# One buffer for both tiles' candidates and the expert numbers, in a decoder layer on one Trainium2 core

## The chip, the core and the metric

The kernel runs on one core of a Trainium2 chip. Its engines each work through a queue of their own, in order: PE (TensorE, the matmuls; its weight loads are listed as PEld), DVE (VectorE), ACT (ScalarE), POOL (GpSimd, which here mostly issues indirect DMAs) and SP, which issues the large DMAs. The metric is the device time of one execution in microseconds (us); smaller is better.

## The reference

One decoder layer over 256 tokens of width 1024: a mixer (gated linear attention and block attention in parallel), and behind it a PEER channel mixer, which the change is in. PEER scores each token against 2 x 128 sub-keys in 8 heads, keeps the best 16 of each half, forms the sums of these pairs, keeps the best 16 of the sums, and with that has 128 experts for each token, of 16,384. The output adds, for each expert, gate times gelu(u_e . x) times v_e.

```python
sv, si = lax.top_k(s, PEER_TOPK)
cand = (sv[:, :, 0, :, None] + sv[:, :, 1, None, :]).reshape(T, PEER_HEADS, 256)
cand_id = (si[:, :, 0, :, None] * PEER_NKEYS + si[:, :, 1, None, :]).reshape(T, PEER_HEADS, 256)
top_s, pos = lax.top_k(cand, PEER_TOPK)
expert = jnp.take_along_axis(cand_id, pos, axis=-1)
gate = jax.nn.softmax(top_s, axis=-1)
# for each token t: sum over its 128 experts of gate * gelu(u_tab[e] . x_t) * v_tab[e]
```

## The kernel before

The tokens are treated in two ways. For tokens 96 to 255 ("many", ND = 160) the kernel multiplies with the whole tables: all 128 blocks of U and then all 128 blocks of V are streamed through TensorE, 512 KB a block (below: a piece), and the product with U is masked by the gates. For tokens 0 to 95 ("few", NS = 96) it gathers only the rows that are needed: 96 indirect DMAs of 512 KB for U and 96 for V, issued by POOL, and one DVE instruction on each.

**Retrieval.** The 256 tokens are two tiles of 128. For each tile `work[tt]` lists the steps on DVE: the best 16 of each half (16 calls of `top16`, each made of MAX, MAX_INDEX, MATCH_REPLACE, MAX, MAX_INDEX, L598 to L602), the pair sums into the tile `cand` (`pairs`, L610 and L613), the best 16 of the sums for each head (8 calls of `top16`, which read and rewrite `cand`), `gates` (a subtraction on DVE, L677, then an exponential on ACT, L678), `ranks` (L622 to L630), for each half `slots` to `slots3` (L637 to L655, ending in the index tile `ij`), and `gates2` (L683 to L685). After the first tile's slots `experts` makes the expert numbers `num` (L669, L670), which POOL writes to DRAM (L566) and reads back spread over the partitions (`ixs`, L573). Only then can POOL issue the gathers (L751), since they take their row numbers from `ixs`. Five buffers (`rowsof`) hold gathered rows. DVE frees one with L759 (U rows) or L769 (V rows). The second tile's retrieval feeds no gather; it is needed by the masks of the many tokens (L801 to L822), which begin at block pair J0 = 31 of U.

**U and V.** In pair `jp` of U TensorE fills one of two PSUM banks named `mm` (L120, two pieces), and ACT empties it with a gelu (L849). So pair jp + 2 cannot begin before ACT has emptied the bank of pair jp. ACT's exponential and its gelu need different function tables, so that a table load (ACT_TABLE_LOAD) stands ahead of each change. Index transposes (L660) and gate transposes (L692) stand between TensorE's matmuls. With V (L890) TensorE sums into three other banks, emptied once at the end (L912). SP fetches pieces in advance into a ring of 14 buffers.

**What sets the order.** The program is written in the order of `work` and of the pairs, and a scheduler then fixes each engine's own order, from the dependencies and from which buffers are free. Buffers come from pools: tiles with the same tag share the pool's slots, and a tile that takes a slot over must wait until every instruction on the tile before it is done, DMAs too. The pool `tk` has one slot for each tag. A tile without a tag goes by its name. So before the change the two `cand` tiles share one slot already, and `num` has a slot of its own.

Of the kernel before, what the change touches and what calls it, by code (L numbers as in the profile page):

```python
# [9 lines left out]
F32 = mybir.dt.float32  # L10
# [3 lines left out]
U32 = mybir.dt.uint32  # L14
# [6 lines left out]
NT = S // 128  # L21
# [8 lines left out]
SLOTS = 128  # L30
# [5 lines left out]
def layer(ctx: ExitStack, tc: tile.TileContext, a):  # L36
# [487 lines left out]
    tk = tk_ctx.enter_context(tc.tile_pool(name="tk", bufs=1))  # L524
# [38 lines left out]
    def to_parts(dst, name, src, cols):  # L563

        there = nc.dram_tensor(name, (NS, src.shape[1]), src.dtype, kind="Internal").ap()
        gp.dma_start(there, src)  # L566
        for l, (t0, n, m) in enumerate(FEW):
            rows = there[t0:t0 + n]
            if cols:
                rows = rows.rearrange("t (m w) -> m t w", m=m)  # L570
            else:
                rows = rows[None].to_broadcast([m, n, src.shape[1]])
            gp.dma_start(dst(l), rows)  # L573

    def by_part(dst):
        return lambda l: dst[:, FEW[l][0]:FEW[l][0] + FEW[l][1]]
# [13 lines left out]
    top = tk.tile([128, NT, 8, 16], F32, name="top")  # L590
    pos = tk.tile([128, NT, 8, 16], U32, name="pos")
    ij = tk.tile([128, 2, NT, 8, 16], F16, name="ij")
    cands = [tk.tile([128, 8, 112], F32, name="cand") for _ in range(NT)]
    later = []
    at = 0

# [7 lines left out]
    def pairs(tt):  # L604


        s0 = sv[:, tt, 0::2]
        s1 = sv[:, tt, 1::2]
        cd = cands[tt]
        ve.tensor_tensor(cd[:, :, 0:64].rearrange("p h (a b) -> p h a b", a=4),  # L610
                         s0[:, :, 0:4, None].to_broadcast([128, 8, 4, 16]),
                         s1[:, :, None, :].to_broadcast([128, 8, 4, 16]), op=OP.add)
        ve.tensor_tensor(cd[:, :, 64:112].rearrange("p h (a b) -> p h a b", a=12),  # L613
                         s0[:, :, 4:16, None].to_broadcast([128, 8, 12, 4]),
                         s1[:, :, None, 0:4].to_broadcast([128, 8, 12, 4]), op=OP.add)
# [47 lines left out]

    def experts():

        num = tk.tile([128, SLOTS], U32, name="num")
        r, c = (ij[:, w, 0].rearrange("p h k -> p (h k)") for w in range(2))
        numf = tk.tile([128, SLOTS], F32, name="numf")
        ve.scalar_tensor_tensor(numf, c, 128.0, r, op0=OP.mult, op1=OP.add)  # L669
        ve.tensor_copy(num, numf)  # L670
        to_parts(by_part(ixs), "experts", num[0:NS], True)
# [33 lines left out]
    for tt in range(NT):  # L705
        w_ = work[tt]
        w_.append((1.8, lambda tt=tt: pairs(tt)))
        w_ += [(1.6, lambda tt=tt, h=h: top16(top[:, tt, h], pos[:, tt, h], cands[tt][:, h])) for h in range(8)]
        st = {}
        w_.append((0.5, lambda tt=tt: gates(tt)))  # L710
        w_.append((3.0, lambda tt=tt, st=st: st.update(ab=ranks(tt))))
        for w in range(2):
            w_.append((1.8, lambda tt=tt, w=w, st=st: st.update(r=slots(tt, w, st["ab"]))))
            w_.append((2.4, lambda st=st: slots2(*st["r"])))
            w_.append((3.0, lambda tt=tt, w=w, st=st: slots3(tt, w, st["r"][0])))
        if tt == 0:
            w_.append((0.6, experts))
        w_.append((0.9, lambda tt=tt: gates2(tt)))
# [264 lines left out]
```

## Time and profile before

| what | us |
|---|---|
| median of 3 runs | 817.42 (817.12 to 818.36) |
| the profiled execution, its own time | 815.44 |
| span of the profiled execution | 813.7 |
| PE busy, share of the span | 98% |
| DVE busy | 61% |
| ACT, POOL busy | 30%, 28% |
| mean granted TensorE clock, as a share of 2.4 GHz | 0.988 |
| DMA over the span | 270 MB, 332 GB/s |

All positions below are us from the start of the span. The retrieval lies at about 160 to 270, the pairs of U at about 200 to 499, V from there to the end. A timeline row gives an instruction's start and length, how many equal ones are merged (x8), and in brackets how long its engine stood idle before it and what it then waited for. Instructions overlap a little, so the step from one start to the next is what one costs in a row. A busy PE is not a PE at its peak, since the ends of matmuls are modelled.

### The profile page before, as it was taken

To read this page: it belongs to the slowest core of one execution; us is meant where nothing else is said; L and a number is where in the kernel's file an instruction comes from. 1 tells how busy PE (TensorE), PEld (TensorE's weight loads), DVE (VectorE), ACT (ScalarE), POOL (GpSimd) and SP (SyncE) were. 2 spreads that over 40 slices of the span, in tenths; PEclk is the share of its full clock that TensorE was granted. 3 is DMA by queue.
4 is the path that set the end of the run, shared out by engine and by line. 5 is a ranking of instruction groups with operands and counts; after the bars stand their busy time and mean duration, and the time that the engine had idled before them with its cause. 6 is when DMAs were issued, how large, how long until landed. Compare 5 with 4: busy or idle time off the path is not lost.

```text
span 813.7 us, 14714 instructions
## 1 busy us (share of the span) xinstructions
PE 794.1 (98%) x5720; PEld 742.7 (91%) x5720; DVE 494.7 (61%) x1073; ACT 242.9 (30%) x645; POOL 230.7 (28%) x257
## 2 busy tenths in 40 slices
PE   8999999999999999999999999999999998999996
PEld 6877579999999999999999999999999988888884
DVE  4796376699995444556676776444555544545554
ACT  6556255543221101687777760000000000000000
POOL 4161010200003333222223234333333333333330
PEclk9998699999999999999999999999999999999999
DMA  9545024878877999999999999999999999999996
GB/s 342 195 140 179 27 78 147 294 187 289 316 241 241 401 408 410 409 407 407 379 361 345 354 381 382 408 410 407 410 408 409 409 409 408 410 409 409 409 408 234
DMA packets 77175, 270.05 MB, mean 332 GB/s; under 512 B 9961, under 2 KB 12025, under 8 KB 76977
## 3 DMA queue, kind: packets, MB, share of 16 engines
q1 hardware_dynamic: 46480, 164.84, 53.9%
q0 software_dynamic: 29616, 102.33, 32.4%
q10 hardware_dynamic: 1008, 1.93, 0.9%
q8 instruction: 45, 0.74, 0.4%
q14 instruction: 26, 0.20, 0.1%
HBM read 266.47 MB, written 2.59 MB: 331 GB/s over the span
## 4 chain that ended last, share of the span: by engine, by line
PE 60%; DMA 27%; DVE 11%; issue 1%; ACT 1%; SPq 0%; DVEq 0%; ACTq 0%
PE mm L120 30%; DMA raw<-in_v_rows 15%; PE sc L890 12%; DMA hi<-in_v_rows 8%; PE mm L69 3%; PE mm L70 3%; PE mm L71 3%; DMA lo<-in_v_rows 3%; PE tr L816 2%; DVE lo L101 2%; PE sc L388 1%; DVE si L602 1%; DVE si L599 1%; DVE scs L600 1%; DVE sv L601 1%
## 5 line engine op out<-in xcount | busy, mean ns | idle before, releaser
L769 DVE SCALAR_TENSOR_TENSOR ys<-rowsof,hs,ys 128x1024 f32<-128x1024 f32 x94 | 120.7, 1284 | 119.2 <-DMA rowsof<-in_v_rows,ixs 119.1
L120 PE MATMUL mm<-yf,raw 128*128 128x160 f32 x1184 | 167.1, 300 | 0.2 <-DMA raw<-in_u 0.2
L120 PEld LDWEIGHTS mm<-yf,raw 128*128 128x128 f32 x1184 | 161.9, 190 | 0.6 <-DMA raw<-in_u 0.5
L759 DVE CUSTOM_DVE_ANT_0 junkd<-rowsof,ys 128x1024 bf16<-128x1024 f32 x96 | 117.3, 1222 | 74.0 <-DMA rowsof<-in_u_rows,ixs 73.7
L751 POOL DMA_INDIRECT rowsof<-in_u_rows,ixs x96 | 97.5, 1016 | 198.3 <-DVE hs L759 182.8
L751 POOL DMA_INDIRECT rowsof<-in_v_rows,ixs x96 | 90.4, 941 | 156.8 <-DVE ys L769 142.7
L805 ACT ACTIVATE B<-E,gf 128x128 f16<-128x128 f16 x320 | 96.7, 388 | 11.1 <-PE tr L816 8.9
L890 PE MATMUL sc<-actB,raw 128*128 128x160 f32 x608 | 91.8, 305 | 4.1 <-DMA raw<-in_v_rows 0.9
L890 PEld LDWEIGHTS sc<-actB,raw 128*128 128x128 f32 x608 | 83.5, 190 | 12.3 <-DMA raw<-in_v_rows 11.4
L890 PE MATMUL sc<-actA,raw 128*128 128x160 f32 x576 | 79.1, 299 | 0.0
L890 PEld LDWEIGHTS sc<-actA,raw 128*128 128x128 f32 x576 | 78.5, 190 | 0.0
L101 DVE TENSOR_TENSOR lo<-raw,hi 128x1024 fp32r<-128x1024 f32 x48 | 58.4, 1223 | 33.0 <-ACT hi L100 33.0
L912 ACT COPY x2d<-sc 128x480 f32<-128x480 f32 (+1 forms) x3 | 1.5, 515 | 240.5 <-PE sc L890 240.5
L100 ACT ACTIVATE hi<-raw 128x1024 fp32r<-128x1024 f32 x48 | 50.7, 1059 | 54.3 <-PE mm L70 23.6
L120 PE MATMUL mm<-yf,hi 128*128 128x160 f32 x432 | 62.4, 301 | 0.0
L120 PE MATMUL mm<-yf,lo 128*128 128x160 f32 x432 | 61.4, 300 | 0.0
L120 PEld LDWEIGHTS mm<-yf,hi 128*128 128x128 f32 x432 | 59.4, 190 | 0.2
L120 PEld LDWEIGHTS mm<-yf,lo 128*128 128x128 f32 x432 | 59.3, 190 | 0.0
L849 ACT ACTIVATE actA<-mm 128x320 f32<-128x320 f32 x32 | 13.9, 436 | 100.5 <-PE mm L120 100.4
L822 DVE SCALAR_TENSOR_TENSOR actA<-tr,actA 128x256 f32<-128x256 f32 x40 | 16.8, 422 | 32.6 <-PE tr L816 32.6
L890 PE MATMUL sc<-actB,lo 128*128 128x160 f32 x224 | 33.8, 305 | 2.6 <-DMA lo<-in_v_rows 1.4
L70 PE MATMUL mm<-qlo,hi 128*128 128x256 f32 x128 | 36.1, 283 | 0.0
(277 smaller groups left out, 1168.2 us busy)
## 6 DMA issues: line engine op xcount, KB each, us to landing
raw<-in_u SPq DMA_DIRECT2D x74, 512.0 KB, 8.6
raw<-in_v_rows SPq DMA_DIRECT2D x74, 512.0 KB, 20.4
hi<-in_u SPq DMA_DIRECT2D x27, 512.0 KB, 7.6
lo<-in_u SPq DMA_DIRECT2D x27, 512.0 KB, 7.5
hi<-in_v_rows SPq DMA_DIRECT2D x27, 512.0 KB, 20.4
lo<-in_v_rows SPq DMA_DIRECT2D x27, 512.0 KB, 20.3
raw<-in_w_rows SPq DMA_DIRECT2D x20, 512.0 KB, 4.0
raw<-in_w_q SPq DMA_DIRECT2D x16, 512.0 KB, 4.8
```

What stands on the lines that cost most here:

```text
L69: pe.matmul(ps, sh, mh, start=first, stop=False)
L70: pe.matmul(ps, sh, ml, start=False, stop=False)
L71: pe.matmul(ps, sl, mh, start=False, stop=last)
L100: sc_.activation(hi, raw, AF.Copy)
L101: ve.tensor_tensor(lo, raw, hi.bitcast(F32), op=OP.subtract)
L120: pe.matmul(ps, rv[:, c], mov[:, c], start=(c == 0), stop=(c == NC - 1))
L751: gp.indirect_dma_start(g, None, a[name], bass.IndirectOffsetOnAxis(ap=ixs[:, k:k + 1], axis=0))
L759: ve.tensor_tensor_reduce(junk, g, ys[place[k]], 1.0, 0.0, OP.mult, OP.add, hs[:, k:k + 1])
L769: ve.scalar_tensor_tensor(sumS, g, hs[:, k:k + 1], sumS, op0=OP.mult, op1=OP.add)
L805: sc_.activation(B[:, k], E[:, k], AF.Copy, scale=gf[:, m, 4 * q + k:4 * q + k + 1])
L822: ve.scalar_tensor_tensor(o, pj[:, j0:d], 1.0 / GS, o, op0=OP.mult, op1=OP.mult)
L890: pe.matmul(acc[c // 3][:, c % 3], raw[:, c * 128:(c + 1) * 128], act[j // 64][:, j % 64], start=False, stop=j == NEXP - 1 and c in (2, 5, 7))
```

## The change

`num` gets the tag of the candidates, and the candidates' tiles are made where they are filled. In program order the slot is now taken by the first tile's `cand`, then by `num`, then by the second tile's `cand`. So the second tile's `pairs` may write only after `num` has been made, and after the DMA that writes `num` to DRAM has landed. No instruction is added or taken away.

```diff
-    cands = [tk.tile([128, 8, 112], F32, name="cand") for _ in range(NT)]
+    cands = {}
...
-        cd = cands[tt]
+
+        cd = cands[tt] = tk.tile([128, 8, 112], F32, name="cand", tag="cand")
...
-        num = tk.tile([128, SLOTS], U32, name="num")
+        num = tk.tile([128, SLOTS], U32, name="num", tag="cand")
```

Line numbers from L609 on are higher by one in the changed kernel: its L611 is L610 of before, its L760 is L759.

The scheduler answers this with other orders on DVE, ACT and, in a few places, PE; POOL and SP keep theirs. On DVE before, these rows stand where the first tile's ranks begin (`rf` is made from `pos`, L625); the second tile's pair sums (L610, L613) and its first scans (L598) are in between.

```order
L625 CAST rf<-pos 128x128
L610 TENSOR_TENSOR cand<-sv 128x8x64
L613 TENSOR_TENSOR cand<-sv 128x8x48
L624 CAST rf<-i_2277 128x256
L683 TENSOR_REDUCE sm<-top 128x8
L598 MAX top<-cand 128x8 x3
L626 SCALAR_TENSOR_TENSOR rf<-rf 128x128
L598 MAX top<-cand 128x8 x2
L684 RECIPROCAL sm<-sm 128x8
L598 MAX top<-cand 128x8 x2
```

Here the second tile is served between the first tile's gates and ranks (L624, L683, L626, L684), and so ahead of `num`.

In the changed kernel the first tile's steps run through to `num`, and only behind it come the second tile's pair sums, L611 and L614.

```order
L654 TENSOR_TENSOR eq<-eq 128x8x64
L654 TENSOR_TENSOR eq<-eq 128x8x32
L656 TENSOR_TENSOR ij<-eq 128x128
L670 SCALAR_TENSOR_TENSOR numf<-ij 128x128
L671 CAST num<-numf 128x128
L611 TENSOR_TENSOR cand<-sv 128x8x64
L614 TENSOR_TENSOR cand<-sv 128x8x48
L598 MAX top<-cand 128x8 x5
L599 MAX_INDEX pos<-top,cand 128x8
L598 MAX top<-cand 128x8 x2
L599 MAX_INDEX pos<-top,cand 128x8
```

So on DVE the second tile's pair sums, its 40 scans and what follows on them have moved from ahead of `num` to behind it.

Further on in the changed kernel, DVE's instructions on gathered rows (printed as ISA, two rows for each gather, `rowsof` being the gathered rows) stand between the second tile's scans. The first gather's two rows stand right ahead of these, and the subtraction ahead of the second tile's exponential (L678, which is L677 of before) comes at their end.

```order
L602 MAX_INDEX pos<-top,cand 128x8
L601 MAX top<-cand 128x8 x2
L602 MAX_INDEX pos<-top,cand 128x8
L601 MAX top<-cand 128x8
L602 MAX_INDEX pos<-top,cand 128x8 x3
L760 ISA junkd,hs<-rowsof,ys 128x1024
L760 ISA hs 128x1
L602 MAX_INDEX pos<-top,cand 128x8 x3
L760 ISA junkd,hs<-rowsof,ys 128x1024
L760 ISA hs 128x1
L678 TENSOR_TENSOR top<-top,mx 128x128
L623 TENSOR_SCALAR i_2919<-pos 128x128
```

Before, that subtraction stands ahead of `num` and so ahead of every gather. It has moved behind the first three gathers.

On ACT before, this is the part from the first tile's exponential (`top`) on, with the gelus that empty the `mm` banks (`actA<-mm`) and the copies of transposed indices (`idxT`):

```order
L678 ACT_TABLE_LOAD
L678 ACTIVATE top<-top 128x128
L849 ACT_TABLE_LOAD
L849 ACTIVATE actA<-mm 128x320 x4
L678 ACT_TABLE_LOAD
L678 ACTIVATE top<-top 128x128
L849 ACT_TABLE_LOAD
L849 ACTIVATE actA<-mm 128x320
L662 COPY idxT<-tr 128x64
L849 ACTIVATE actA<-mm 128x320 x2
L662 COPY idxT<-tr 128x64
L849 ACTIVATE actA<-mm 128x320
```

and this is the same part of the changed kernel:

```order
L679 ACT_TABLE_LOAD
L679 ACTIVATE top<-top 128x128
L850 ACT_TABLE_LOAD
L850 ACTIVATE actA<-mm 128x320 x5
L663 COPY idxT<-tr 128x64
L850 ACTIVATE actA<-mm 128x320 x2
L663 COPY idxT<-tr 128x64
L679 ACT_TABLE_LOAD
L679 ACTIVATE top<-top 128x128
L850 ACT_TABLE_LOAD
L850 ACTIVATE actA<-mm 128x320
```

The second tile's exponential and its two table loads have moved from behind the eighth gelu to behind the eleventh, ahead of the twelfth.

PE's order in this part stays but for one index transpose, which moves two matmuls forward; the second tile's transposes keep their places. From pair 31 on gathers and masks are interleaved differently on DVE: ahead of the last multiplication with `gl` (L853, the end of the masks) stand 71 of the 96 U gathers before, and 74 in the changed kernel.

## Rows read from the trace of the kernel before

**Rows 1.** the page, part 4: the chain that ended last, share of the span by engine

```profile
PE 60%; DMA 27%; DVE 11%; issue 1%; ACT 1%; SPq 0%; DVEq 0%; ACTq 0%
```

**Rows 2.** windows: us, busy (x instructions) by engine, clock, DMA share, GB/s

```profile
500.00:550.00 50.00, 50.00 (x361) 48.99 (x360) 25.03 (x42) 0.00 (x0) 20.55 (x20) 1.00 1.03 409
650.00:700.00 50.00, 46.65 (x310) 42.28 (x309) 24.31 (x20) 0.00 (x0) 17.79 (x19) 1.00 1.03 409
```

**Rows 3.** waits of SP's queue from 440 to 500: total us, times, longest

```profile
SPq L94 <- PE mm L120: 48.1, 23, 2.8
```

**Rows 4.** timeline of DVE: start us, us, instruction, count [idle before <-releaser]

```profile
213.16 1.50 DVE L598 MAX8 top<-cand 128x8 f32<-128x112 f32 x8
...
222.05 0.29 DVE L677 TENSOR_TENSOR top<-top,mx 128x128 f32<-128x128 f32 x1
...
222.66 0.68 DVE L610 TENSOR_TENSOR cand<-sv 128x512 f32<-128x512 f32 x1
...
223.73 0.28 DVE L624 CAST rf<-i 128x256 f32<-128x256 uint32 x1
...
246.24 1.22 DVE L638 TENSOR_TENSOR eq<-iot,ab 128x2048 f16<-128x2048 f16 x1
247.38 0.22 DVE L670 CAST num<-numf 128x128 uint32<-128x128 f32 x1
```

**Rows 5.** timeline of POOL, the DMAs that it issues

```profile
247.89 0.54 POOL L566 DMA_DIRECT2D experts<-num  x1 [14.05 <-DVE num L670]
252.38 1.46 POOL L573 DMA_DIRECT2D ixs<-experts  x2 [3.96 <-DMA experts<-num]
258.66 1.08 POOL L751 DMA_INDIRECT rowsof<-in_u_rows,ixs  x1 [4.82 <-DMA ixs<-experts]
```

**Rows 6.** timeline of DVE at the first gathered rows; then the landing of all gathers

```profile
267.04 1.23 DVE L759 CUSTOM_DVE_ANT_0 junkd<-rowsof,ys 128x1024 bf16<-128x1024 f32 x1 [11.89 <-DMA rowsof<-in_u_rows,ixs]
...
271.81 1.23 DVE L759 CUSTOM_DVE_ANT_0 junkd<-rowsof,ys 128x1024 bf16<-128x1024 f32 x1 [0.87 <-DMA rowsof<-in_u_rows,ixs]
...
DMA to landing us min/median/max: 6.1/11.1/13.0
```

**Rows 7.** timeline of ACT, exponentials between evictions

```profile
238.75 0.31 ACT L678 ACTIVATE top<-top 128x128 f32<-128x128 f32 x1 [3.39 <-DVE top L677]
239.08 1.28 ACT L849 ACT_TABLE_LOAD   x1
240.37 0.44 ACT L849 ACTIVATE actA<-mm 128x320 f32<-128x320 f32 x1
...
252.84 0.44 ACT L849 ACTIVATE actA<-mm 128x320 f32<-128x320 f32 x1 [3.92 <-PE mm L120]
...
257.30 0.44 ACT L849 ACTIVATE actA<-mm 128x320 f32<-128x320 f32 x1 [3.43 <-PE mm L120]
```

**Rows 8.** timeline of PE, index transposes and the first matmuls with V

```profile
239.91 0.23 PE L660 MATMUL tr<-identh,ij 128*128 128x128 f16 x1 [1.44 <-DVE ij L655]
...
317.95 0.22 PE L660 MATMUL tr<-identh,ij 128*128 128x128 f16 x1
...
499.73 8.18 PE L890 MATMUL sc<-actA,raw 128*128 128x160 f32 x59
```

**Rows 9.** TensorE's clock: a row of PE's timeline, then windows

```profile
89.31 0.79 PE L69 MATMUL mm<-hi,xhi 128*128 128x512 f32 x1
...
90.00:95.00 5.00, 5.00 (x18) 3.58 (x16) 0.00 (x0) 0.44 (x2) 0.00 (x0) 0.59 0.01 3
...
811.00:812.00 1.00, 0.00 (x0) 0.00 (x0) 0.00 (x0) 0.00 (x0) 0.00 (x0) 0.50 0.64 213
```

**Rows 10.** timeline at the end: weight loads of two pieces, last gathers on DVE

```profile
795.82 2.20 PEld L890 LDWEIGHTS sc<-actB,raw 128*128 128x128 f32 x16 [0.30 <-DMA raw<-in_v_rows]
...
800.90 2.20 PEld L890 LDWEIGHTS sc<-actB,raw 128*128 128x128 f32 x16 [0.26 <-DMA raw<-in_v_rows]
...
801.43 3.93 DVE L769 SCALAR_TENSOR_TENSOR ys<-rowsof,hs,ys 128x1024 f32<-128x1024 f32 x3 [0.74 <-DMA rowsof<-in_v_rows,ixs]
```

## The prediction

> **The bound.** I read the chain of waits first, for what sets the end: 60% of the span is TensorE, 27% DMA, 11% DVE [rows 1]. The windows then show where each holds. While U runs and into V TensorE is the bound: from 500 to 550 it is still busy for the whole 50.00 us [rows 2]. Later the two DMA streams are the bound: from 650 to 700 both still move 409 GB/s, but TensorE does 310 instructions where it did 361 [rows 2]. Third, SP's waits, for which of the two paces the stream just before V: from 440 to 500 SP's queue stands 48.1 of 60 us waiting for TensorE to free a ring buffer [rows 3]. So the ring is full when V begins, and V begins when TensorE has finished U. A delay of TensorE in U is therefore a delay of V's start with the same full ring. Only then come the timelines of DVE, POOL, ACT and PE around the retrieval, since that is where the change moves instructions.
>
> **Taken away.** Between the first tile's last scan and `num` DVE now also does the second tile's pair sums and scans. Forty scans and a small copy take 222.05 - 213.16 = 8.9 us on the first tile, pair sums 223.73 - 222.66 = 1.1, the subtraction and three small steps 222.66 - 222.05 = 0.6, the large comparison 247.38 - 246.24 = 1.1 [rows 4]; nine more small steps of gates and ranks at some 0.17 each (an estimate between 0.6 / 4 and the 0.22 of the last row) are 1.5. That is 13.2 us; I take 13.0, because the first tile's dependent steps lose their fillers. `num`, now done at 247.6, is done at 234.6. The chain behind it stays as it is: experts to DRAM, back, first gather, first gathered rows on DVE are at 247.89, 252.38, 258.66 and 267.04 [rows 5, 6], and so at 234.9, 239.4, 245.7 and 254.0.
>
> TensorE gets something at once: its first index transpose waits 1.44 us for DVE now [rows 8], at 239.9, and with the first tile served first its index is there some ten us earlier. Term one: -1.4 us.
>
> **Added: DVE.** The second tile's pair sums may write only when the DMA of `num` has landed, at about 239.4: 4.7 us of standing still. All of the second tile is queued behind it, but work of some 7 us (two pair sums, 27 scans at 8.9 / 40 = 0.22 each) then brings DVE to its first gathered rows at 246.6, and those land at 254.0. The wait of 11.9 us that stands there now [rows 6] hides it; without that cover it would cost the 4.7. I cost it at nothing.
>
> **Added: ACT.** The second tile's subtraction now stands behind three gathers on DVE, and its exponential stands ahead of ACT's twelfth gelu. ACT works in order. So the bank of TensorE's twelfth pair is not emptied before three gathers have landed. The third gathered rows come 271.81 - 267.04 = 4.8 us after the first [rows 6], at 258.8; DVE's own work up to there (two gathers of 1.23, eleven scans at 0.22) ends at 258.9, so both say the same. Then 1.23 for the third, 0.3 for the subtraction, and from the start of the exponential to the end of the gelu 240.37 + 0.44 - 238.75 = 2.1 [rows 7]: 258.9 + 1.2 + 0.3 + 2.1 = 262.5, say 262.6. When does TensorE want that bank? The twelfth gelu starts at 252.84 and the thirteenth at 257.30 [rows 7]; with two banks TensorE enters the pair after that when the thirteenth pair is done, at 257.1, and 1.4 earlier with term one, at 255.7. Term two: TensorE stands still from 255.7 to 262.6, +6.9 us. Before, the same exponential stood behind the eighth gelu and held up the ninth until 240.37 [rows 7], which blocked nothing, because the second bank covers a pair's length of 4.5 us. Now the cover is too short by the 6.9.
>
> The table load between exponential and gelu takes 1.28 us, and the gelu starts at 240.37, right at its end [rows 7]. [...]
>
> **The clock.** No row shows dense matmuls after a pause of 7 us, so I bound this. At the end of the kernel, with TensorE out of work, the granted clock falls to 0.50 (1.2 of 2.4 GHz) [rows 9]. At 89.31 dense matmuls start at that level, and from 90 to 95 the mean is 0.59, so (1 - 0.59) / 0.5 x 5 = 4.1 us of that stretch are at half [rows 9]: 4.8 us in all, of which half is lost, 2.4. The ends are 0 (the clock holds) and some 3.4 (half as long again). I take term three at +2.3 us, since an idle engine lost its clock in the one place where the trace has one. [...]
>
> **Gathers.** In masks and U DVE's order ties the gathers to TensorE's pace, so their 13 us shrink to the three gathers by which the new order is ahead at the end of U (74 against 71). In V gathers and stream share the DMA evenly: a piece of the stream arrives every (800.90 - 795.82) / 2 = 2.54 us [rows 10], which is half of 409 GB/s. So gathers ahead do not speed the stream up; they only end 3 x 2.55 = 7.7 us sooner in relation to it. At present the last ones on DVE (801.43 to 805.4) end with the last piece (800.90 + 2.20) [rows 10], so in the last 7.7 us TensorE would get its pieces without sharing, at its own 2.20 instead of 2.54: 3.0 pieces x 0.34. Term four: -1.0 us. Behind the last piece nothing changes (eviction, three output DMAs, the residual rows).
>
> Nothing else comes late: the second tile's transposes are wanted at 317.95 [rows 8], and its last index is ready after eleven gathers, at about 254 + 10 x 2.6 = 280. That the stream's ring runs dry while the gathers run freely ahead of the masks I cost at nothing too: they begin 13 us earlier, but the pause refills the ring. If it did run dry, the 13 us hold five pieces at 2.54 instead of 2.20, 1.7 us.
>
> **The sum.** -1.4 + 6.9 + 2.3 - 1.0 = +6.8 us. On the profiled execution that is a span of 813.7 + 6.8 = 820.5 and a time of 815.44 + 6.8 = 822.2. The median of the runs is 1.98 above that execution, so I predict 817.42 + 6.8 = 824.2 us, 0.8% slower. A measurement of this kernel can tell about 0.2% (1.6 us) from no change.
>
> **Rivals.** *The delay is swallowed in V (faster).* From 650 on TensorE idles for the stream. If the stream were bound by DMA alone since before V's start, a TensorE that is late would cost nothing, and three gathers of 512 KB moved into idle DMA time would save 3 x 1.28 = 3.8: 813.6. For it speaks 409 GB/s all through V [rows 2]; against it the 48.1 us in which SP waits for TensorE before V [rows 3]. It decides if the ring is not full when V begins.
>
> *No pause (faster).* If the exponential ran before 253.3, ACT would be back in time, and terms one and four alone would stay: 817.42 - 2.4 = 815.0. That needs the third gather 7 us sooner than the DMA chain of rows 5 and 6 gives it; nothing in the trace is that much quicker.
>
> *Half a pause (no change).* If gathers land about 4 us sooner, because the DMA is emptier at 246, and the clock holds: -1.4 + 2.9 - 1.0, 817.9.
>
> *More pauses (slower still).* From pair 31 on the new order puts one mask instruction behind the next one-hot on DVE, so a bank of the masks may be freed later, and the ring may run dry for the 1.7 us above: with 2 us for the masks some 4 us more, 828.
>
> **Numbers.** The forecast gets 0.76, more pauses 0.09, the swallowed delay 0.05, no pause 0.05, half a pause 0.05. Slower by over 0.2% is 0.76 + 0.09 = 0.85; within 0.2% 0.05; faster 0.05 + 0.05 = 0.10. For the first gather's landing, 8.4 us after its issue (267.04 - 258.66), the bounds are the quickest of all gathers, 6.1, and the median, 11.1 [rows 6]. The low end takes the clock's 0 and the 6.1: 824.2 - 2.3 - 2.3 = 819.6; the high end the clock's 3.4 and the 11.1: 824.2 + 1.1 + 2.7 = 828.0. The forecast and most of the longer pauses lie in it, some 0.8.
>
> **Signs.** In the changed profile: `num` at about 234.6 and the first gather at 245.7; DVE waiting for the DMA of `num` ahead of L611; no wait ahead of the first index transpose; ACT's second exponential after some 12 us of idle time; TensorE standing about 7 us at 256, released by ACT, then at half clock for 4 to 5 us; V's first matmul at about 507 instead of 499.73 [rows 8]; the last gather several us ahead of the last piece. I am wrong if TensorE's pause is missing or far from 7 us, or if V's late start does not reach the end.

## The result, and the profile after

The changed kernel takes 824.5 us (median of six runs, 823.2 to 828.0) where the kernel before takes 817.1. The ratio is 1.0102, with a 95% interval from 1.0078 to 1.0126: slower by about 1%. The prediction said 824.2.

One thing has to be known for reading the rows. The execution in the profile of after took 828.0 us (span 826.2), the longest of the six, and a second one, taken later, 828.1 (span 826.4). The two of before are of executions below their median (spans 813.7 and 812.7). So the profiles lie 12.5 to 13.7 us apart and the medians 7.4.

The chain by engine (part 4 of the profile's page) says little yet: as in [rows 1], mostly TensorE and DMA.

```profile
PE 57%; DMA 30%; DVE 9%; ACT 1%; issue 1%; POOL 1%; SPq 0%; DVEq 0%; ACTq 0%
```

DVE and POOL around the retrieval, timelines of after, to set beside [rows 4 to 6]:

```profile
238.12 0.23 DVE L671 CAST num<-numf 128x128 uint32<-128x128 f32 x1
242.57 0.69 DVE L611 TENSOR_TENSOR cand<-sv 128x512 f32<-128x512 f32 x1 [4.22 <-DMA experts<-num]
...
258.17 1.23 DVE L760 CUSTOM_DVE_ANT_0 junkd<-rowsof,ys 128x1024 bf16<-128x1024 f32 x1 [8.04 <-DMA rowsof<-in_u_rows,ixs]
...
261.09 1.20 DVE L760 CUSTOM_DVE_ANT_0 junkd<-rowsof,ys 128x1024 bf16<-128x1024 f32 x1
...
262.96 1.21 DVE L760 CUSTOM_DVE_ANT_0 junkd<-rowsof,ys 128x1024 bf16<-128x1024 f32 x1
...
264.10 0.29 DVE L678 TENSOR_TENSOR top<-top,mx 128x128 f32<-128x128 f32 x1
```

```profile
238.64 0.54 POOL L566 DMA_DIRECT2D experts<-num  x1 [5.03 <-DVE num L671]
242.76 1.46 POOL L573 DMA_DIRECT2D ixs<-experts  x2 [3.58 <-DMA experts<-num]
250.40 1.08 POOL L752 DMA_INDIRECT rowsof<-in_u_rows,ixs  x1 [6.18 <-PE tr L661]
```

`num` comes at 238.12, 9.3 us earlier than before. The second tile's pair sums wait 4.22 us for its DMA (L611), and then DVE waits 8.04 us all the same for the first gathered rows. Three gathers stand ahead of the subtraction L678.

ACT, timeline of after, to set beside [rows 7]:

```profile
249.57 0.44 ACT L850 ACTIVATE actA<-mm 128x320 f32<-128x320 f32 x1 [3.91 <-PE mm L120]
...
250.13 1.28 ACT L679 ACT_TABLE_LOAD   x1
264.42 0.31 ACT L679 ACTIVATE top<-top 128x128 f32<-128x128 f32 x1 [13.01 <-DVE top L678]
264.74 1.28 ACT L850 ACT_TABLE_LOAD   x1
266.04 0.44 ACT L850 ACTIVATE actA<-mm 128x320 f32<-128x320 f32 x1
```

Behind its eleventh gelu (249.57) ACT loads the exponential's table and stands for 13.01 us until DVE's subtraction is done. The twelfth gelu starts at 266.04. What TensorE makes of that, timeline of PE in after:

```profile
227.42 13.31 PE L120 MATMUL mm<-yf,raw 128*128 128x160 f32 x96 [0.86 <-ACT actA L850]
240.56 0.22 PE L661 MATMUL tr<-identh,ij 128*128 128x128 f16 x1
...
253.94 4.51 PE L120 MATMUL mm<-yf,lo 128*128 128x160 f32 x32
```

```profile
266.53 19.15 PE L120 MATMUL mm<-yf,raw 128*128 128x160 f32 x128 [8.08 <-ACT actA L850]
```

At 240.56 the index transpose no longer waits (1.44 us in [rows 8]). From 258.4 to 266.53 TensorE stands, 8.08 us, released by ACT. The 128 matmuls behind that take 19.15 us; the same row of before reads 17.55. Windows of after over the stop, columns as in [rows 2]; the granted clock is the third number from the right:

```profile
261.00:263.00 2.00, 0.00 (x0) 0.00 (x0) 2.00 (x10) 0.00 (x0) 0.43 (x1) 0.95 1.03 420
263.00:265.00 2.00, 0.00 (x0) 0.00 (x0) 1.84 (x7) 0.57 (x2) 1.05 (x2) 0.50 1.03 418
...
269.00:271.00 2.00, 2.00 (x15) 2.00 (x14) 2.00 (x7) 0.00 (x0) 0.92 (x1) 0.85 1.04 395
271.00:273.00 2.00, 2.00 (x17) 2.00 (x16) 2.00 (x5) 0.33 (x1) 0.47 (x1) 1.00 0.97 346
```

The clock falls to 0.50 during the stop and is back at 1.00 about 3 us after the matmuls resume (0.85 over 269 to 271 puts it at 269.6, an estimate from that row). Last, the end, timelines of weight loads and of DVE, to set beside [rows 10]:

```profile
808.80 2.20 PEld L891 LDWEIGHTS sc<-actB,raw 128*128 128x128 f32 x16 [0.28 <-DMA raw<-in_v_rows]
811.35 4.37 PEld L891 LDWEIGHTS sc<-actB,raw 128*128 128x128 f32 x32 [0.34 <-issue]
```

```profile
811.65 1.28 DVE L770 SCALAR_TENSOR_TENSOR ys<-rowsof,hs,ys 128x1024 f32<-128x1024 f32 x1 [1.21 <-DMA rowsof<-in_v_rows,ixs]
```

The last gather ends at 812.9, the last two pieces come back to back and end at 815.7. Before, the last gather ended at 805.4, 2.3 us behind the last piece at 803.1 [rows 10].

### The profile page after: what moved, and what is told of

It is laid out like the page before. It is cut to its first block, busy times and chain, and to the rows that moved or that the text cites. A ratio compares the mean times of both kernels' runs of the same rounds, so it can differ in the third digit from the quotient of the medians.

```text
span 826.2 us, 14717 instructions
## 1 busy us (share of the span) xinstructions
PE 798.1 (97%) x5720; PEld 744.9 (90%) x5720; DVE 494.4 (60%) x1073; ACT 242.7 (29%) x645; POOL 231.6 (28%) x257
## 3 DMA queue, kind: packets, MB, share of 16 engines
HBM read 266.47 MB, written 2.59 MB: 326 GB/s over the span
## 4 chain that ended last, share of the span: by engine, by line
PE 57%; DMA 30%; DVE 9%; ACT 1%; issue 1%; POOL 1%; SPq 0%; DVEq 0%; ACTq 0%
PE mm L120 30%; DMA raw<-in_v_rows 17%; PE sc L891 9%; DMA hi<-in_v_rows 8%; PE mm L69 3%; PE mm L70 3%; PE mm L71 3%; DMA lo<-in_v_rows 3%; PE tr L817 2%; DVE lo L101 1%; PE sc L388 1%; DVE si L602 1%; DVE si L599 1%; DVE scs L600 1%; DMA rowsof<-in_u_rows,ixs 1%
## 5 line engine op out<-in xcount | busy, mean ns | idle before, releaser
L752 POOL DMA_INDIRECT rowsof<-in_u_rows,ixs x96 | 101.2, 1054 | 208.8 <-DVE hs L760 180.2
L760 DVE CUSTOM_DVE_ANT_0 junkd<-rowsof,ys 128x1024 bf16<-128x1024 f32 x96 | 117.3, 1221 | 58.2 <-DMA rowsof<-in_u_rows,ixs 58.0
L891 PEld LDWEIGHTS sc<-actB,raw 128*128 128x128 f32 x608 | 83.5, 190 | 14.5 <-DMA raw<-in_v_rows 13.7
L71 PE MATMUL mm<-qhi,lo 128*128 128x256 f32 x128 | 36.3, 285 | 0.1
L69 PE MATMUL mm<-qhi,hi 128*128 128x256 f32 x128 | 36.0, 282 | 0.0
```

Source lines behind the costliest of these rows:

```text
L69: pe.matmul(ps, sh, mh, start=first, stop=False)
L71: pe.matmul(ps, sl, mh, start=False, stop=last)
L752: gp.indirect_dma_start(g, None, a[name], bass.IndirectOffsetOnAxis(ap=ixs[:, k:k + 1], axis=0))
L760: ve.tensor_tensor_reduce(junk, g, ys[place[k]], 1.0, 0.0, OP.mult, OP.add, hs[:, k:k + 1])
L891: pe.matmul(acc[c // 3][:, c % 3], raw[:, c * 128:(c + 1) * 128], act[j // 64][:, j % 64], start=False, stop=j == NEXP - 1 and c in (2, 5, 7))
```

## The experiments

The kernel before was run beside each group, at 816.3 to 816.7 us. "The stop" is TensorE's wait ahead of pair 14.

**The changed kernel again.** No edit.

> The changed kernel once more, to see which part of the profile shown is its own and which belongs to that one execution. Theory: TensorE's pause ahead of pair 14 of U is there again and measures 7.5 to 8.5 us, the 128 matmuls behind it take about 19.2 us instead of 17.6, and V begins some 8 to 9 us later than before (about 508). V takes 303.4 us as before or up to 1 us less, so the profiled execution ends near 822, and the median of the runs is again about 824.5. Rival: V itself is longer in the changed kernel, 305 us or more as in the profile shown, and then a part of the loss lies in V and not in the pause.

826.1 us (822.7 to 828.2), 1.0103 of before (1.0068 to 1.0138). Timeline of PE:

```profile
264.21 20.10 PE L120 MATMUL mm<-yf,raw 128*128 128x160 f32 x128 [7.75 <-ACT actA L850]
```

The stop is there, 7.75 us, and the clock costs 20.10 - 17.55 = 2.55, some 0.9 more than expected. V's first matmul is at 508.76, against 499.05 before ([rows 8] show it cut at the window's start). But V to the end of the span is 317.6 us where before it is 314.65: the rival was right in part.

**Without the second exponential.** ACT's stop taken away, all else left.

```diff
-        sc_.activation(gt, gt, AF.Exp)
+        if tt == 0:
+            sc_.activation(gt, gt, AF.Exp)
```

> The changed kernel, leaving out the exponential of the second tile's gates (so the gates of tokens 128 to 255 are not a softmax). DVE and POOL keep the changed order; ACT has nothing left in U that waits for a gather. Theory (the pause on ACT is the whole loss): no pause of TensorE around 258 to 266, clock at 1.00 there, and 824.5 - 8.1 - 1.6 = 814.8 us, which is also 1.4 + 1.0 below the kernel before. Rival (the loss sits in the new order of DVE and of the gathers: the wait for the DMA of the expert numbers, or a longer V): little changes, 821 to 825 us.

816.4 us, 0.9992 of before (0.9979 to 1.0004). Timeline of PE at the place of the stop:

```profile
256.26 17.55 PE L120 MATMUL mm<-yf,raw 128*128 128x160 f32 x128
```

No stop, no loss of clock, and with that one instruction the whole loss against before is gone. But the kernel is not 2.4 us faster than before, as the sum wanted; V is 317.2 us here, as long as in the changed kernel.

**Four banks.** The exponential stays late, but TensorE has more banks to go on with (cover).

```diff
-        pv = bank("mm")[:, :2 * ND]...
+        pv = bank("sc" if jp < 24 and jp % 4 > 1 else "mm")[:, :2 * ND]...
```

> The changed kernel, whole, but pairs 2, 3, 6, 7, ... 22, 23 of U take their PSUM bank from the four banks of the tag sc, which stand idle there, so that TensorE can go on for three more pairs (some 13 us) while ACT waits. Theory (two banks are what makes ACT's wait a pause of TensorE): the exponential comes as late as in the changed kernel, ACT's 13 us wait stays, and TensorE has no pause: 814.8 us. If only the bank count mattered a little and TensorE is stopped by something else that waits for ACT (a transpose, say), a pause of 2 to 8 us stays: 817 to 825. Rival (loss elsewhere, in DVE's order or in V): 822 to 825 us.

816.2 us, 1.0002 of before (0.9986 to 1.0018). Timeline of ACT, then all that PE waited for from 200 to 520:

```profile
263.81 0.31 ACT L679 ACTIVATE top<-top 128x128 f32<-128x128 f32 x1 [14.21 <-DVE top L678]
```

```profile
PE sc L120 <- DMA raw<-in_u: 0.5, 1, 0.5
```

ACT stands even longer, 14.21 us, and TensorE does not notice. So here a late ACT costs nothing by itself (816.2 us); with two banks it was a stop of 8.08 us.

**Gates ahead of the gathers.** The subtraction is put ahead of the gathers: the maximum that it needs (`mx`) takes the one buffer into which DVE's gather instruction writes, and the program writes the first gather only behind the second tile's gates.

```diff
-        mx = tk.tile([128, 8], F32, name="mx")
+        mx = (gat if tt else tk).tile([128, 8], F32, name="mx", tag="junkd" if tt else "mx", bufs=1)
...
-            few_to((jp - j1 + 1) * 2 * NS // (64 - j1 + 61))
+            if len(work[1]) <= 8:
+                few_to((jp - j1 + 1) * 2 * NS // (64 - j1 + 61))
```

> The changed kernel, whole, but the second tile's maximum (the small copy ahead of the subtraction) is put into the one buffer into which DVE's gather instructions write, and the first gather is written behind the second tile's gates. So the subtraction stands ahead of all gathers on DVE instead of behind three. Num still shares the candidates' slot, and the wait for its DMA stays. Theory: pair sums at 242.6, 40 scans of 8.9 us and the sums 1.1, so the subtraction at about 252.8 instead of 264.1, gelu at about 255, a pause of about 1.2 us instead of 8.1 and no fall of the clock: 824.5 - 8.1 - 1.6 + 1.2 = 816.0 us. Rival (loss in V or in the first tile first order): 822 to 825 us.

817.7 us, 1.0012 of before (0.9994 to 1.0030). Timelines of DVE and PE:

```profile
241.24 0.69 DVE L611 TENSOR_TENSOR cand<-sv 128x512 f32<-128x512 f32 x1 [4.30 <-DMA experts<-num]
...
251.33 0.29 DVE L678 TENSOR_TENSOR top<-top,mx 128x128 f32<-128x128 f32 x1
```

```profile
253.77 4.61 PE L120 MATMUL mm<-yf,lo 128*128 128x160 f32 x32 [1.07 <-ACT actA L850]
```

The subtraction comes 12.8 us earlier than in after, the stop shrinks to 1.07 us, and the 32 matmuls behind it take 0.1 more (4.61 - 4.51). DVE still waits 4.30 us for the DMA of `num`, so this wait isn't the loss. Again the time is 1.7 us above what was expected, as it was 1.6 and 1.4 above in the two runs before.

**The kernel before again.** No edit; for V.

> The kernel before, once more, for a second profile of its V. In the first profile the stream of V got 4.9 pieces' worth of bytes in the first 10 us of V, against 3.9 to 4.3 in the four profiles of changed kernels, and from there on stream and gathers share the DMA evenly in all of them. Theory (the head start is a property of the order): again 4.6 to 5.0 pieces, and V to the end of the span 314 to 315.3 us. Rival (it was that execution's luck): 3.9 to 4.3 pieces, and 316 to 317.6 us.

V to the end is 314.9 us, as in the first profile. The hardware queue (the stream of pieces, and `x2d`, one load of 0.66 MB at V's start) in the first 10 us of V, before again and changed kernel again (packets, MB, share):

```profile
q1 hardware_dynamic: 648, 2.50, 62.1%
```

```profile
q1 hardware_dynamic: 524, 2.05, 55.4%
```

Counted in pieces of 0.524 MB that is 4.8 against 3.9, with `x2d` in both. All profiles with 14 buffers in the ring and five for gathers, those of later runs too, in one table (us; MB of the same queue line; the first three have the order of before):

| kernel | V's first matmul | end of span | V to the end | MB in V's first 10 us |
|---|---|---|---|---|
| before | 499.05 | 813.7 | 314.7 | 2.59 |
| before again | 497.79 | 812.7 | 314.9 | 2.50 |
| before with a stop | 509.55 | 824.2 | 314.7 | 2.60 |
| after | 510.13 | 826.2 | 316.1 | 2.27 |
| after again | 508.76 | 826.4 | 317.6 | 2.05 |
| without the second exponential | 498.27 | 815.5 | 317.2 | 2.04 |
| four banks | 499.03 | 815.7 | 316.7 | 2.03 |
| gates ahead of the gathers | 500.22 | 816.5 | 316.3 | 2.25 |
| without the wait for the DMA | 510.67 | 826.3 | 315.6 | 2.29 |
| one bank more | 502.87 | 819.0 | 316.1 | 2.06 |

From 10 us on the two queues move nearly the same in all of them, 15.5 to 15.7 pieces each per 40 us. From V's start to the end the hardware queue moves 62.5 to 62.6 MB in every one of them, so the ring is equally full when V begins. So the theory holds: in the changed orders the stream lacks 0.4 to 1.1 pieces of head start, and V is 0.7 to 3.0 us longer.

**The kernel before with a stop.** Only a stop is added; the order of the retrieval is that of before.

```diff
+        if k == 2:
+            sc_.copy(junk[:, 0:8], g[:, 0:8])
```

> The kernel before with one instruction more: ACT copies eight columns of the third gathered rows, so that ACT stands until the third gather has landed, while the order of DVE and of the gathers stays. The copy stands behind ACT's twelfth gelu. Theory (a stop of ACT in U goes one to one to the end, whatever the retrieval's order): the thirteenth gelu waits until about 272.3, TensorE wants its bank at 261.6, so it stands for 11.0 us, the clock costs 2 to 2.6 more, and the kernel takes 817 + 13.5 = 830.5 us (828 to 833). Rival (a late start of V is swallowed in V, where TensorE later idles for the stream): 817 to 820 us.

826.2 us, 1.0109 of before (1.0068 to 1.0150). Timelines of ACT and PE:

```profile
269.57 0.20 ACT L760 CAST junkd<-rowsof 128x8 bf16<-128x8 f32 x1 [16.37 <-DVE hs L761]
```

```profile
270.16 15.00 PE L120 MATMUL mm<-yf,raw 128*128 128x160 f32 x96 [9.21 <-ACT actA L851]
```

The stop is 9.21 us, not 11.0, because the third gathered rows were there at 269.6 and not at 271.8. The clock takes 15.00 - 13.31 (96 matmuls at full clock) = 1.7. V's first matmul is at 509.55 and the span ends at 824.2: V takes 314.65 us, as before, so V swallows nothing of the delay. The expected time was 4.3 us too high (1.8 of it the stop, some 0.8 the clock, the rest open), the mechanism right.

**Without the wait for the DMA of `num`.**

```diff
-        num = tk.tile([128, SLOTS], U32, name="num", tag="cand")
+        num = tk.tile([128, SLOTS], U32, name="num")
-        numf = tk.tile([128, SLOTS], F32, name="numf")
+        numf = tk.tile([128, SLOTS], F32, name="numf", tag="cand")
```

> The changed kernel, but the numbers in float (numf, the tile from which num is made) take the candidates' slot in place of num, which has a slot of its own again. So the order of the three tiles stays, and DVE no longer waits 4.2 us for the DMA of num. Then one gather instead of three stands ahead of the second tile's subtraction, and the exponential stands ahead of ACT's eleventh gelu instead of its twelfth. Theory (that wait is hidden under the wait for the first gathered rows): DVE's wait ahead of the first rows grows from 7.75 to about 12 us, the exponential comes at about 258 instead of 262, but its gelu is also wanted one pair (4.4 us) sooner, so TensorE stands for about 8 us and the time stays at 823 to 827 us. Rival (the DMA wait is part of the loss): 820 us or less.

826.4 us, 1.0103 of before (1.0061 to 1.0145): as slow as after. Timelines of DVE and PE:

```profile
239.16 0.69 DVE L611 TENSOR_TENSOR cand<-sv 128x512 f32<-128x512 f32 x1
...
257.13 1.22 DVE L760 CUSTOM_DVE_ANT_0 junkd<-rowsof,ys 128x1024 bf16<-128x1024 f32 x1 [8.40 <-DMA rowsof<-in_u_rows,ixs]
```

```profile
261.33 7.49 PE L120 MATMUL mm<-yf,lo 128*128 128x160 f32 x32 [6.46 <-ACT actA L850]
```

The pair sums follow `num` at once, and DVE waits for the first gathered rows just the same, 8.40 us (not 12: it first does scans that stood behind the gathers). The stop is 6.46 us, and the clock costs 7.49 - 4.51 = 3.0. So taking away the wait for the DMA of `num` gains nothing. The run also changes the order, so that its time alone does not price that wait; the run with the gates ahead of the gathers, which keeps a wait of 4.30 us and takes 817.7 us, says the same.

**One bank more, for one pair.**

```diff
+        pv = bank("sc" if jp == 12 else "mm")[:, :2 * ND]...
```

> The changed kernel, whole, but one pair of U, the thirteenth, takes a bank of the tag sc instead of mm. So TensorE has cover for one pair of 4.4 us more while ACT waits for three gathers. Theory (the pause is ACT's lateness less the cover of the banks): the pause falls from 7.75 to 3.3 us (3.0 to 3.8) and comes one pair later; the clock costs somewhere between 0 and 2.5, and the time lies between the two and the four bank kernels: 816.2 + 3.3 + 1.2 = 820.7 us (819 to 822.5). Rival (the pause does not depend on the banks by the pair's length): 824 or 816 us.

821.1 us, 1.0069 of before (1.0046 to 1.0093): between the two, as expected. The profile doesn't show the split that was expected. Timeline of PE:

```profile
227.30 14.98 PE L120 MATMUL mm<-yf,raw 128*128 128x160 f32 x96 [1.87 <-ACT actA L850]
...
264.55 13.31 PE L120 MATMUL mm<-yf,raw 128*128 128x160 f32 x96 [0.20 <-ACT actA L850]
```

In this execution the first tile's exponential came late (225.19 against 223.32 in after again) and made a stop of its own, 1.87 us plus 14.98 - 13.31 = 1.7 of clock. TensorE was then 3.5 us later than in after again when it came to this place, and the stop there shrank from the expected 3.3 to 0.2. The sum is about the same, but that a pair of cover takes 4.4 us off the stop is not shown by this run.

**One piece more in the ring.** Does the stream's head start set V's end? Three runs.

> The changed kernel with four PSUM banks as in the run of that name, and the ring of pieces holds 15 buffers instead of 14; the gathers have four buffers instead of five. Theory (in V the end is set by how many pieces the stream has in hand when the even sharing of the DMA begins, and one piece is 2.5 us): 816.2 - 2.5 = 813.7 us, which is below both kernels, with stream and gathers still sharing evenly in V. Rival (four buffers starve the gathers, or V is bound by them): 816 us or more, with the last gather behind the last piece.

> The changed kernel with four PSUM banks, and a ring of 15 pieces instead of 14, with the five gather buffers kept (the run with one piece more took one of them for it). DVE's order is that of the kernel with four banks. There the gathers end some 3 us before the last piece. Theory (V ends with whichever of the two comes last, the stream's share of the DMA being fixed by even sharing, and one piece in hand is worth 2.5 us to the stream): the stream's end moves up to the gathers' end, 816.2 - 2.5 = 813.7 us (813.2 to 814.7), below both kernels. Rival (the ring is not what the stream lacks): 815.5 to 817 us.

> The kernel before with a ring of 15 pieces instead of 14, nothing else. There the last gathers already end with or behind the last piece. Theory (V ends with whichever comes last): the stream comes 2.5 us sooner, the gathers do not, and the last gathers hold the end: 816.5 us, within 0.8 of the kernel before. Rival (the stream alone sets V's end): 814.1 us.

The edit to the ring, the same in all three (the first two also have the edit for four banks, and the first sets `bufs=4` for `rowsof`):

```diff
-    ... + [("raw2", 3, gat)] * 3
+    ... + [("raw2", 4, gat)] * 4
```

With four gather buffers the time is 819.2 us (1.0027, 1.0004 to 1.0051): the rival's forecast. DVE's last gather:

```profile
806.36 1.28 DVE L770 SCALAR_TENSOR_TENSOR ys<-rowsof,hs,ys 128x1024 f32<-128x1024 f32 x1 [4.59 <-DMA rowsof<-in_v_rows,ixs]
```

It lands 4.59 us after DVE was free, long after the stream's last weights are loaded (797.7): now the gathers hold V. With all five buffers kept, on the changed order with four banks, it is 813.5 us, as the theory said: 0.9972 of before (0.9957 to 0.9986), faster than both kernels. On the kernel before it is 813.9 (0.9971, 0.9955 to 0.9988), where I had expected 816.5: this is the rival's time. The chain of waits names a gather near the end:

```profile
798.10 6.65 DMA rowsof<-in_v_rows,ixs
804.79 3.46 DMA res<-x_rows
```

The timelines of SP's queue and of DVE in the same run don't bear that step out:

```profile
802.65 1.78 SPq L913 DMA_DIRECT2D out<-x2d  x3
804.79 0.33 SPq L901 DMA_DIRECT2D res<-x_rows  x1
```

```profile
808.35 1.28 DVE L907 TENSOR_TENSOR res<-res,mm 96x512 f32<-96x512 f32 x2 [1.90 <-DMA res<-x_rows]
```

SP issues the load of `res` (the residual rows) right behind the three output DMAs, which wait for the stream's last sums, and DVE's last addition then waits 1.90 us for `res`. In before the same two rows stand at 802.61 and 804.60. So here too the stream's end sets V's end, as the rival has it. Against V's start the last piece ends 2.2 us sooner than in before and the gathers 1.2 us sooner. V to the end is 312.5 us there (314.7 without), and 314.3 with four banks (316.7 without): a piece in hand is worth 2.2 to 2.4 us in either order.

## Why the prediction was right, point by point

- **The bound.** Right. A delay of TensorE in U reaches the end one to one: the stop put into the kernel before moved V's first matmul from 499.05 to 509.55 and did not change V's length, 314.7 us.
- **Taken away.** 13 us less ahead of `num` were predicted, and `num` came 9.3 us earlier. In this execution the retrieval itself ran later (the first tile's subtraction is at 224.98, before at 222.05), which is 2.9 of the missing 3.7. Term one, -1.4, is there in every profile of the changed order: no transpose waits.
- **DVE's new wait** (4.7 predicted, 4.22 measured): free, as costed: without it the time is the same (826.4 us), and with it but with a stop of only 1.07 us nearly nothing is lost (817.7).
- **ACT and the stop.** The place, the releaser and the two banks were right. The size was 6.9 predicted, 8.08 and 7.75 measured. TensorE wanted the bank at 258.4 and 256.5 instead of 255.7, and the gelu was done some 4 and 2 us later than the predicted 262.5. Taking the stop away, by four banks, saves 8.3 to 9.9 us (against 824.5 and 826.1); the two terms were 9.2 together. The table load behaved as the rows had said: exponential at 264.42, load at 264.74, gelu at 266.04, 1.28 us.
- **The clock**, +2.3: measured +1.6, +2.55, +1.7 and +3.0 after the stops of 8.08, 7.75, 9.21 and 6.46 us. In after and after again the clock stands at 0.50 when the matmuls resume (from 263 to 269, matmuls from 266.53; from 260 to 268, matmuls from 264.21); +1.7 and +3.0 are the longer time of the matmuls behind the other two stops, put down to the clock. After the stop of 1.87 us in the run with one bank more the burst began at 1.00 and fell to 0.50 some 0.7 us later. The estimate of 2.4 taken from [rows 9] lies within what was measured.
- **Gathers**, -1.0: this step failed, and with the wrong sign. Its first half is there: the gathers end 2.8 us ahead of the last piece where before they ended 2.3 behind it (the prediction read these two as one time), a shift of 5.1 us and not 7.7, and the last two pieces come at 2.2 us each. What the step left out is the start of V. It assumed that from V's start stream and gathers share evenly. That holds only from some 10 us on. In the kernel before, DVE was held up by masks while gathers landed; at V's start it did five in a row (500.1 to 506.4). From 503 to 507 the gathers' queue (q0) moved 0.3 of one gather's bytes and the stream's queue (q1) 2.9 pieces, and so the stream got ahead (lines below the list). In the new order the gathers run a little ahead (three in a row at V's start), the gap is smaller, and the stream has 0.4 to 1.1 pieces less. A piece is worth 2.2 to 2.4 us (the ring of 15). So the term was +0.7 to +3.0 instead of -1.0. That the gap stems from DVE's order is read from the timelines only; no run changes it alone. Nor is it the whole account: in the first 10 us of V both queues together move 4.0 to 4.1 MB in the order of before and only 3.3 to 3.8 MB in the changed ones, so the DMA has time to spare there. Why the stream does not use it stays open.

The DMA queues of the kernel before from 503 to 507, for the last point:

```profile
q1 hardware_dynamic: 379, 1.50, 91.9%
q0 software_dynamic: 43, 0.16, 9.9%
```

The two wrong sizes, a stop about 1 us too short and V about 3 us too short, are both on one side, and yet the median came within 0.3 us of the forecast. By the profiles' terms the loss is -1.4 + 7.9 + 2.1 + 2 = 10.6 us, which fits the runs near 828, not those near 823. Of the six runs of after the two above 827 have a mean granted clock of 0.983 and the three below 824 one of 0.986, but the sixth, at 825.2, has the lowest, 0.982: so the clock is at most a part of the difference. No run near 823 has a profile: where their loss is smaller stays open, and the closeness of the median is in part luck.

## What to carry to other kernels

When tiles are made to share a buffer, look for what the new order puts behind a DMA on each engine in turn: here the wait that the sharing adds was free (4.22 us, with another of 8.04 for the first gathered rows behind it), and the loss came from an instruction two engines away, queued in order ahead of the one that empties a PSUM bank (a stop of 8.08 us). Four banks took the stop away here, and the small instruction moved ahead of the first wait for gathered rows left 1.07 us of it. In V, where two streams shared the DMA evenly for a long stretch (15.5 to 15.7 pieces each per 40 us), the time to the end was 0.7 to 3.0 us longer when the needed stream had 0.4 to 1.1 pieces less in its first 10 us; a buffer more in its ring was worth 2.2 to 2.4 us in either order.

## What the runs showed of the hardware that was not expected

**Gather issue beside DVE.** An issue of a gather on POOL takes 0.94 us in 172 of 192 cases in before and in 171 in after, but up to 2.85. Timelines of POOL and of DVE in after:

```profile
272.53 2.85 POOL L752 DMA_INDIRECT rowsof<-in_u_rows,ixs  x1 [2.61 <-DVE gf L701]
...
281.06 2.75 POOL L752 DMA_INDIRECT rowsof<-in_u_rows,ixs  x1 [2.39 <-DVE hs L760]
...
288.22 1.80 POOL L752 DMA_INDIRECT rowsof<-in_u_rows,ixs  x1 [1.13 <-DVE hs L760]
```

```profile
272.29 2.28 DVE L644 TENSOR_TENSOR eq<-eq,sif 128x2048 f16<-128x2048 f16 x1
...
280.70 2.29 DVE L644 TENSOR_TENSOR eq<-eq,sif 128x2048 f16<-128x2048 f16 x1
...
287.98 1.22 DVE L760 CUSTOM_DVE_ANT_0 junkd<-rowsof,ys 128x1024 bf16<-128x1024 f32 x1
```

Each of these began some 0.3 us after a DVE instruction with two inputs in SBUF and ended 0.8 us after that one's end (272.29 + 2.28 + 0.8 = 275.4 = 272.53 + 2.85; the other two alike). In the traces of before and after all issues of over 1 us except the very first of each (1.08), 30 in sum, end 0.80 to 0.82 us after the end of a DVE instruction with two inputs in SBUF that had begun 0.14 to 0.69 us ahead of them. Two that began 0.01 and 0.02 us after the start of such a one (450.80 in before, 431.73 in after) took 0.94. The 30 issues that began during L822 (L823 in after), of whose two inputs one, `tr`, lies in PSUM, took 0.93 to 0.94 us, with up to 0.42 us of that instruction still to come. So some issues were held up beside DVE, as far as the timing of the rows shows; no run takes the DVE instruction away, and what holds them is not shown. Nothing shows that it cost time here.

**A stop of 1.9 us cost as much clock as one of 9.2.** After the 1.87 us in the run with one bank more, 96 matmuls took 1.7 us longer, as after the 9.21 us. After the stop of 0.86 us (after, 227.42) 96 took 13.31 us, with no loss. Windows of the run with one bank more:

```profile
227.00:228.00 1.00, 0.70 (x5) 0.71 (x6) 1.00 (x1) 0.57 (x2) 0.54 (x1) 0.99 0.94 348
228.00:229.00 1.00, 1.00 (x6) 1.00 (x5) 1.00 (x3) 0.00 (x0) 0.00 (x0) 0.50 0.47 162
```

The clock fell when the matmuls, back since 227.30, were already running again.
